# The last directly computed projection of an encoder layer becomes two seven-product units, and the attention steps beside it are packed closer

## The chip, the cores and the metric

The kernel runs on one core of a Trainium2 chip. The metric is the device time of one execution in microseconds. Before the change it is 2159.87 us, the median of 3 runs (2159.56 to 2159.9).

The engines carry these names in the profile: PE (TensorE, matrix products; PEld its weight loads), DVE (VectorE), ACT (ScalarE), POOL (GpSimd, which here mostly issues DMAs) and SP (SyncE, which only issues DMAs).

## The reference

One layer of an encoder, 512 tokens, width 2048, all in float32:

```python
h = rmsnorm(x, attn_norm_w)
aq, ak, av, gq, gk, gv, gr, glr = split(h @ w_in)        # widths 1024 x3, 512, 512, 1024, 1024, 32
attn = mixture_of_dilations(aq, ak, av, rel_table)       # 16 heads x 64: softmax over a banded set of keys + bias
o = gla_forward(gq, gk, gv, glr) + gla_backward(...)     # 4 "linear" heads, dk=128, dv=256, chunked scan with gates
gla_out = rmsnorm_per_head(o) * gla_norm_w * silu(gr)
x = x + concat(attn, gla_out) @ w_out
h = rmsnorm(x, ffn_norm_w)
x = x + (silu(h @ w_gate) * (h @ w_up)) @ w_down         # hidden width 5632
return rmsnorm(x, final_norm_w)
```

The part that matters here is the projection `h @ w_in`, and in it the columns of `gq` and `gk`, 512 each: the queries and keys of the four linear heads.

## The kernel before, in words

**Products.** Every float32 product is made of three products of rounded parts: each operand is split into a high part `hi` (a rounded copy, by ACT) and a low part `lo` (the rest, by DVE), and `hi*hi + hi*lo + lo*hi` is summed in PSUM. The kernel has two ways to compute a projection.

- A *direct job* (`job`, `run_job`) makes 512 output columns for 512 tokens. It goes over the 16 slices of the inner dimension; for each it loads a weight slice (`Stream.load`, on SP), splits it (`Stream.split` on ACT, `Stream.rests` on DVE), and for each of four PSUM banks issues three matmuls of 128x512. That is 16 x 4 x 3 = 192 matmuls a job. Between the banks it advances *side work* by steps: `rate` steps for one slice, taken from a queue of generators (`run_side`). One `yield` in such a generator ends one step.
- A *seven-product unit* (`Feed`, `Front`) makes 256 output columns for 512 tokens by a scheme of Strassen's kind: seven products of block sums in place of eight. A unit has four pieces, a piece has 14 products, and each of these is one matmul of 128x512 (L1562) and one of 128x256 (L1548). The sums of weight blocks (`Blocks.sums`) and the parts (`Blocks.split`) cost DVE and ACT time ahead of it; afterwards `evac7` puts the seven results together with ACT copies, DVE additions and four accumulating DMAs from GpSimd.

**Order of the program around the change.** First two direct jobs make the values `av` (to 104 us). Then `Front.run` computes 14 units: four of `gr`, one each of the first 256 columns of `gq` and `gk`, and eight of `aq` and `ak` (104 to 378 us). Then come three direct jobs: one of kind "A" for the other 256 columns of `gq` and of `gk` (lines L337 to L339), and two of kind "B" for `gv` (L346 to L348). Beside these three jobs, as side work at `RATES[0]` = 3.1 steps a slice, the gates' low-rank projection and then the whole of `attention` are done. After them come the direct jobs of `w_out` at 4.0 steps a slice (603 to 831 us), beside which `gla` computes the linear heads; then the feed-forward layer in seven-product units (`Feed`, to 1695 us) and in `Down`.

**The attention generator.** It has 64 *units of attention* `u` (16 heads, 4 blocks of 128 queries), and 71 iterations of two steps each, since the stages of a unit are spread over iterations like a pipeline. For unit `u`: in iteration `u`, first step, PE makes the scores (`att_scores`, L630 and L631); in the second step DVE adds the bias and finds the extreme (`att_max`, L640). In iteration `u+1`, first step, ACT takes the exponential (`att_exp`, L648). In iteration `u+2`, second step, DVE takes the reciprocal of the sum (L651) and, for even `u`, scales the tile by it (L653). In `u+3`, first step, ACT scales the tile for odd `u` (L657); second step: PE transposes it (L662). In `u+4`, ACT rounds the transposed tile (`att_round`, L670) in the first step, DVE takes the rest (`att_rest`, L676) in the second. Then come the product with the values (L686, L687), `att_lift` (ACT, L696) and `att_mix` (DVE, L705). Every engine works through its own queue in the order in which the instructions were written. Four of the eight PSUM banks belong to the direct job; the attention units share the other four, so the scores of a unit need a bank that DVE has emptied.

**Queries and keys.** `aq` and `ak` lie in DRAM (`qkd`). For each pair of heads `read_qk` (L569) issues eight DMAs from the GpSimd queue, all at once in the iteration with `u % 8 == 1`; `load_qk` then makes their parts on ACT (L592) and DVE (L588), four times each for eight units of attention.

**Linear heads.** `evac_gqk` (L854 to L859) scales the results of the job of kind "A" and stores them in `gqd`; the first 256 columns come from the units through `gfd`. `load_gla` reads them back from GpSimd's queue.

## Time and profile before

| what | value |
|---|---|
| median of 3 runs | 2159.87 us |
| profiled execution | 2159.02 us, of which the span of instructions is 2157.2 us |
| granted PE clock in that execution | 0.999 |
| PE busy | 2145.5 us, 99% of the span |
| DVE, ACT, POOL busy | 1843.6, 1234.4 and 364.0 us |

PE's busy time counts a matmul until its modelled end, and matmuls overlap, so their own rate is read from the distance between the starts of neighbours. DVE and ACT instructions that follow one another overlap a little too: the sum of the durations of a group of them is some per cent more than the busy time of the engine. A time of idleness that is put down to a releaser ("<-PE ps L631") says whose end came last before the waiting instruction started.

### The profile page before, as it was taken

What the parts mean: (1) busy time and instruction counts of PE and PEld (TensorE: products, weight loads), DVE (VectorE), ACT (ScalarE), POOL (GpSimd) and SP (SyncE); (2) the same over time, 40 slices, a digit from 0 to 9 for tenths busy, and PEclk for the clock granted to TensorE, in tenths of its full rate; (3) what the DMA queues carried; (4) which work ended last, traced back from release to release, by engine and by line L of the source; (5) the groups of instructions that cost most, each with busy time, mean ns of one, the idle gap of its engine ahead of it and who ended that gap; (6) DMA issues with size and microseconds to landing.
All of it is one profiled execution on the core that took longest, in us unless ns stands there. A gap on an engine that the chain in (4) does not pass through costs nothing.

```text
span 2157.2 us, 35082 instructions
## 1 busy us (share of the span) xinstructions
PE 2145.5 (99%) x12714; PEld 1896.6 (88%) x12714; DVE 1843.6 (85%) x3187; ACT 1234.4 (57%) x2250; POOL 364.0 (17%) x501
## 2 busy tenths in 40 slices
PE   9999999999999999999999999999999999999998
PEld 7888888888888889888888888888888899999987
DVE  6699999688878788899999998999989888888885
ACT  8455555578876456455555555555555655555562
POOL 0011222211121110022112211221122220021300
PEclk9999999999999999999999999999999999999999
DMA  6367778846575863567677667776677885576982
GB/s 203 136 181 182 179 179 192 245 143 190 174 220 172 279 243 103 149 181 182 181 179 196 173 183 182 178 194 174 180 188 181 260 212 178 179 183 156 282 309 78
DMA packets 266203, 407.55 MB, mean 189 GB/s; under 512 B 19309, under 2 KB 163613, under 8 KB 266030
## 3 DMA queue, kind: packets, MB, share of 16 engines
q1 hardware_dynamic: 206238, 274.59, 39.8%
q0 software_dynamic: 59472, 130.19, 27.1%
q8 instruction: 100, 1.64, 0.3%
q14 instruction: 73, 0.60, 0.1%
q10 hardware_dynamic: 320, 0.53, 0.1%
HBM read 287.47 MB, written 66.39 MB: 164 GB/s over the span
## 4 chain that ended last, share of the span: by engine, by line
PE 56%; DMA 1%; issue 1%; DVE 1%; POOL 0%; ACT 0%; DVEq 0%; ACTq 0%; POOLq 0%
PE ps L1562 25%; PE ps L1548 12%; PE ps L1926 5%; PE ps L1927 5%; PE ps L1925 5%; PE ps L346 1%; PE ps L348 1%; PE ps L347 1%; PE ps L2122 1%; PE ps L2121 1%; PE ps L2120 1%; DMA gd<-b 1%; DMA b<-a 0%; POOL xd L1806 0%; DVE b L1471 0%
## 5 line engine op out<-in xcount | busy, mean ns | idle before, releaser
L1466 ACT CAST b<-b 128x1024 fp32r<-128x1024 f32 (+1 forms) x585 | 533.8, 944 | 386.4 <-DVE b L1471 193.1
L1471 DVE TENSOR_TENSOR b<-b,b 128x1024 fp32r<-128x1024 f32 (+1 forms) x585 | 614.0, 1084 | 34.4 <-ACT b L1466 22.9
L1562 PE MATMUL ps<-b,b 128*128 128x512 f32 x1708 | 500.7, 393 | 0.4 <-ACT b L1466 0.2
L1562 PE MATMUL ps<-a,b 128*128 128x512 f32 x1428 | 418.7, 393 | 0.3 <-DVE b L1582 0.2
L1562 PEld LDWEIGHTS ps<-b,b 128*128 128x128 f32 x1708 | 289.4, 188 | 32.6 <-ACT b L1466 0.6
L1548 PEld LDWEIGHTS ps<-b,b 128*128 128x128 f32 x1708 | 280.6, 190 | 40.8
L1548 PE MATMUL ps<-b,b 128*128 128x256 f32 x1708 | 307.4, 280 | 0.0
L1548 PEld LDWEIGHTS ps<-a,b 128*128 128x128 f32 x1428 | 236.9, 189 | 38.0 <-DVE b L1471 0.5
L1562 PEld LDWEIGHTS ps<-a,b 128*128 128x128 f32 x1428 | 238.5, 188 | 24.1 <-issue 0.6
L1548 PE MATMUL ps<-a,b 128*128 128x256 f32 x1428 | 256.6, 280 | 0.1
L1453 DVE TENSOR_TENSOR b<-b 128x512 f32<-128x512 f32 x268 | 183.6, 685 | 19.0 <-PE ps L1927 7.3
L1926 PE MATMUL ps<-b,b 128*128 128x256 f32 x624 | 176.6, 283 | 0.0
L1927 PE MATMUL ps<-b,b 128*128 128x256 f32 x624 | 176.6, 283 | 0.0
L1925 PE MATMUL ps<-b,b 128*128 128x256 f32 x624 | 176.6, 283 | 0.0
L346 PE MATMUL ps<-b,b 128*128 128x512 f32 x332 | 133.8, 403 | 0.1
L348 PE MATMUL ps<-b,b 128*128 128x512 f32 x332 | 129.8, 391 | 0.1
L347 PE MATMUL ps<-b,b 128*128 128x512 f32 x332 | 129.5, 390 | 0.0
L1454 DVE TENSOR_TENSOR b<-b,b 128x256 f32<-128x256 f32 x268 | 114.0, 425 | 9.3
L1455 DVE TENSOR_TENSOR b<-b,b 128x256 f32<-128x256 f32 x268 | 114.0, 425 | 9.2
L1927 PEld LDWEIGHTS ps<-b,b 128*128 128x128 f32 x624 | 119.8, 192 | 0.0
L1925 PEld LDWEIGHTS ps<-b,b 128*128 128x128 f32 x624 | 119.8, 192 | 0.0
L1926 PEld LDWEIGHTS ps<-b,b 128*128 128x128 f32 x624 | 119.8, 192 | 0.0
(308 smaller groups left out, 4039.8 us busy)
## 6 DMA issues: line engine op xcount, KB each, us to landing
b<-in_w_gate_dram SPq DMA_DIRECT2D x109, 512.0 KB, 3.7
b<-in_w_up_dram SPq DMA_DIRECT2D x88, 512.0 KB, 3.8
b<-in_w_down_dram SPq DMA_DIRECT2D x88, 512.0 KB, 5.4
b<-in_w_in_dram SPq DMA_DIRECT2D x86, 512.0 KB, 3.8
b<-a POOLq DMA_DIRECT2D x168, 256.0 KB, 4.5
b<-in_w_out_dram SPq DMA_DIRECT2D x32, 512.0 KB, 6.3
gd<-b POOLq DMA_DIRECT2D x22, 512.0 KB, 4.0
b<-gd SPq DMA_DIRECT2D x22, 512.0 KB, 8.3
```

What stands on the lines that cost most here:

```text
L346: mm(o, xh.t[:, c], wh.t[:, w], start=first and not on, stop=False, skip_group_check=on)
L347: mm(o, xh.t[:, c], wl.t[:, w], start=False, stop=False, skip_group_check=on)
L348: mm(o, xl.t[:, c], wh.t[:, w], start=False, stop=last, skip_group_check=on)
L1453: dve.tensor_tensor(s_[:, :, 0:2], r[:, :, 1:3], r[:, :, 0:1].to_broadcast(shape), op=OP.add)
L1454: dve.tensor_tensor(s_[:, :, 2], s_[:, :, 0], r[:, :, 2], op=OP.add)
L1466: act.copy(o, src)
L1471: dve.tensor_tensor(o, src, h, op=OP.subtract)
L1548: mm(o, wl, xh, start=False, stop=end, skip_group_check=True)
L1562: mm(o.rearrange("p (s t) -> p s t", s=2), wh, x_, start=first and p == 0, stop=False, skip_group_check=True)
L1925: mm(o, xh[:, t], wh, start=first and h == 0, stop=False, skip_group_check=True)
L1926: mm(o, xh[:, t], wl, start=False, stop=False, skip_group_check=True)
L1927: mm(o, xl[:, t], wh, start=False, stop=last, skip_group_check=True)
```

## The change

- **Projection.** The direct job of kind "A" and `evac_gqk` are gone. `Front` has two more units, the second 256 columns of `gq` and of `gk`, as its units 6 and 7; `aq` and `ak` follow. So there are 16 units and then two direct jobs (`gv`). `gfd` has four parts, and `load_gla` reads all heads from it.
- **Rate.** `RATES[0]`, the steps of side work for one slice in the jobs of `gv`, is 4.4 in place of 3.1. The generators `low_rank` and `attention`, and `load_qk(0)`, `load_v(0)` and the late store of the last unit, hang on the first job of `gv`.
- **Scaling.** `att_norm` is called for unit `u-1` at the end of the second step of iteration `u` (before: for `u-2`, at the head of the second step), and `att_scale` for `u-2` (before `u-3`). Who multiplies the tile by the reciprocal: ACT for `u % 4 == 2`, and for odd `u` below 8; GpSimd for the other odd units, 28 in number; DVE for `u % 4 == 0`. Before, DVE had the 32 even ones and ACT the 32 odd ones.
- **Transfers.** `read_qk` is a generator that issues one DMA and yields; `attention` calls it twice an iteration, from `u % 8 == 0` on, so that the eight DMAs of a pair lie in four iterations. `scan_operands` (two memsets and four DMAs on GpSimd) is paced in the same way and starts at `u == 43` in place of 47.

```diff
                         for r in (slice(0, 64), slice(64, 128)):
                             pool.dma_start(out=qkr[pr][i][n].f[r], in_=src)
+                            yield
...
         def att_norm(u):
             dve.reciprocal(ar[u % 4], asum[u % 4])
-            if u % 2 == 0:
-                dve.tensor_scalar(AT[u].t, AT[u].t, ar[u % 4], None, op0=OP.mult)
+            if not by_act(u):
+                e = pool if u % 2 else dve
+                e.tensor_scalar(AT[u].t, AT[u].t, ar[u % 4], None, op0=OP.mult)
+
+        def by_act(u):
+            return u % 4 == 2 or u % 2 and u < 8
 
         def att_scale(u):
-            if u % 2:
+            if by_act(u):
                 act.activation(AT[u].t, AT[u].t, AF.Copy, scale=ar[u % 4])
...
-                    if u % 8 == 1:
-                        read_qk(h // 2 + 1)
+                    if u % 8 == 0:
+                        for _ in reads:
+                            pass
+                        reads = read_qk(h // 2 + 1)
+                    next(reads, None)
...
                 run(att_scores, u)
-                run(att_scale, u - 3)
+                run(att_scale, u - 2)
                 run(att_round, u - 4)
                 run(att_exp, u - 1)
...
                 yield
-                run(att_norm, u - 2)
+                next(reads, None)
                 run(att_transpose, u - 3)
...
                     run(att_mix, (u - 7) // 2, UNITS // 2)
+                run(att_norm, u - 1)
...
-        RATES = (3.1, 4.0)
+        RATES = (4.4, 4.0)
         APART = 12
-        seg = [(w_in, C_GQ + 256), (w_in, C_GK + 256)]
-        job("A", [piece512(seg, None, k) for k in range(0, KT, 2)], list(range(KT)), acts_h,
-            evac_gqk, rate=RATES[0], start=gstart, before=before_first, limit=3)
         for pr in range(2):
             j = job("B", [piece512(w_in, C_GV + pr * 512, k) for k in range(0, KT, 2)], list(range(KT)), acts_h,
-                    evac_gv(pr), rate=RATES[0],
-                    before=(lambda i: load_gates() if i == 12 else None) if pr else None)
+                    evac_gv(pr), rate=RATES[0], start=None if pr else gstart, limit=3,
+                    before=(lambda i: load_gates() if i == 12 else None) if pr else before_first)
...
                 self.units = [(w_in, C_GR + g * 256) for g in range(4)] + [(w_in, C_GQ), (w_in, C_GK)] + \
+                    [(w_in, C_GQ + 256), (w_in, C_GK + 256)] + \
                     [(w_in, c + g * 256) for g in range(4) for c in (C_AQ, C_AK)]
...
-                    if u == 4:
+                    if u in (4, 6):
                         dve.scalar_tensor_tensor(c_.t, c_.t, P ** -0.5, r, op0=OP.mult, op1=OP.mult)
                     else:
                         dve.tensor_tensor(c_.t, c_.t, r, op=OP.mult)
-                    pool.dma_start(out=grd[u] if u < 4 else gfd[u - 4] if u < 6 else qkd[u - 6], in_=c)
+                    pool.dma_start(out=grd[u] if u < 4 else gfd[u - 4] if u < 8 else qkd[u - 8], in_=c)
```

In the tables of instruction order below, a row gives the line, the operation, what it writes and reads (`a` and `b` are SBUF tiles of 512 and 1024 columns, `ps` PSUM banks, `small` the per-row numbers) and its size. After the change L641 is `att_max`, L652 and L655 are `att_norm`, L681 is `att_rest`, L710 is `att_mix`.

In DVE's queue, two units of attention in the middle of that stage, before:

```order
L651 RECIPROCAL small<-small 128x1
L653 TENSOR_SCALAR a_252_4969<-a_252_4969,small 128x512
L676 TENSOR_TENSOR b_496_5023<-ps_198_5004,b_495_5022 128x4x128
L640 ISA a_263_5052,small<-ps_199_5018,b_488_4864 128x512
L640 ISA small 128x1
L651 RECIPROCAL small<-small 128x1
L676 TENSOR_TENSOR b_496_5023<-ps_200_5037,b_495_5022 128x4x128
L640 ISA a_265_5077,small<-ps_202_5060,b_488_4864 128x512
L640 ISA small 128x1
L705 TENSOR_TENSOR a_251_4932<-ps_201_5042,a_264_5065 64x2x128
```

The same place in DVE's queue after the change:

```order
L681 TENSOR_TENSOR b_541_5230<-ps_205_5237,b_540_5229 128x4x128
L641 ISA a_250_5274,small<-ps_207_5260,b_536_5147 128x512
L641 ISA small 128x1
L710 TENSOR_TENSOR a_243_5211<-ps_206_5242,a_249_5265 64x2x128
L652 RECIPROCAL small<-small 128x1
L655 TENSOR_SCALAR a_248_5252<-a_248_5252,small 128x512
L218 TENSOR_TENSOR a_241_5198<-b_526_4910,a_240_5197 128x512
L681 TENSOR_TENSOR b_544_5293<-ps_208_5268,b_543_5292 128x4x128
L641 ISA a_253_5315,small<-ps_209_5289,b_536_5147 128x512
L641 ISA small 128x1
```

The rest and the maximum now stand ahead of the reciprocal, and of two scalings by DVE in four units one is left.

In GpSimd's queue, the stores of the direct job's results and the reads of a pair of heads, before:

```order
L859 DMA gqd<-a_219_4669 128x512
L569 DMA a_222_4685<-qkd 64x512 x2
L569 DMA a_223_4686<-qkd 64x512 x2
L569 DMA a_224_4687<-qkd 64x512 x2
L569 DMA a_225_4688<-qkd 64x512 x2
```

After the change, in GpSimd's queue where its first scaling stands (that of unit 9):

```order
L569 DMA a_186_4679<-qkd 64x512 x2
L569 DMA a_187_4680<-qkd 64x512 x2
L569 DMA a_188_4681<-qkd 64x512 x2
L655 ISA
L655 TENSOR_SCALAR a_192_4737<-a_192_4737,small 128x512
L569 DMA a_189_4682<-qkd 64x512 x2
L655 TENSOR_SCALAR a_197_4802<-a_197_4802,small 128x512
L655 TENSOR_SCALAR a_206_4869<-a_206_4869,small 128x512
L569 DMA a_215_4946<-qkd 64x512 x2
L655 TENSOR_SCALAR a_213_4936<-a_213_4936,small 128x512
```

Scalings now stand between the DMA issues, and ahead of the first of them there is one instruction without operands (the row `L655 ISA`), by which GpSimd loads the code that the scaling needs. It stands there once in the program.

33 lines of the change are left out of this document (13 added, 20 removed).

## The prediction

> **What bounds the kernel now.** I read the page's busy times first, then the table by stretches, since the change touches two stages only.
>
> ```profile
> PE 2145.5 (99%) x12714; PEld 1896.6 (88%) x12714; DVE 1843.6 (85%) x3187; ACT 1234.4 (57%) x2250; POOL 364.0 (17%) x501
> ...
> 104.00:377.00 273.00, 272.73 (x1564) 239.14 (x1563) 251.28 (x399) 143.94 (x236) 57.65 (x74) 1.00 0.74 183
> 399.00:596.00 197.00, 196.84 (x1095) 167.39 (x1094) 166.68 (x395) 155.00 (x330) 35.08 (x67) 1.00 0.57 172
> 596.00:831.00 235.00, 234.15 (x1142) 196.61 (x1141) 184.00 (x392) 139.20 (x308) 39.77 (x69) 1.00 0.68 221
> ```
>
> The columns are the stretch, its length, and the busy times of PE, PEld, DVE, ACT and POOL; then clock, DMA share, GB/s. The three stretches are the front units, the attention beside direct jobs, and the linear heads beside `w_out`. PE is without a pause in all of them, at full clock. So a matmul saved is time saved, as long as the others keep up: DVE is at 92% in the front (251.28 of 273), at 85% in the attention (166.68 of 197), ACT there at 79%.
>
> How fast matmuls follow each other stands in the timeline, which gives starts. Two matmuls of the direct job that goes away with one between them, two of a later direct job with twenty between them, and the first matmuls of the first and of the last front unit:
>
> ```profile
> 380.00 0.39 PE L337 MATMUL ps<-b,b 128*128 128x512 f32 x1
> ...
> 380.46 0.39 PE L339 MATMUL ps<-b,b 128*128 128x512 f32 x1
> ...
> 610.65 0.40 PE L346 MATMUL ps<-b,a 128*128 128x512 f32 x1
> ...
> 615.42 0.39 PE L346 MATMUL ps<-b,a 128*128 128x512 f32 x1
> ...
> 104.24 0.62 PE L1562 MATMUL ps<-b,b 128*128 128x512 f32 x2
> ...
> 358.45 0.63 PE L1562 MATMUL ps<-b,b 128*128 128x512 f32 x2
> ```
>
> A direct matmul takes 0.23 us from start to start ((380.46 - 380.00) / 2); over 21 of them it is (615.42 - 610.65) / 21 = 0.227, which I use, since the longer row rounds less. A front unit takes (358.45 - 104.24) / 13 = 19.55 us.
>
> **Term 1: PE.** Away go 192 direct matmuls: 192 x 0.227 = 43.6 us. New are two units: 2 x 19.55 = 39.1 us. Everything else on PE (scores, transposes, values, low-rank) keeps its count. Sum: -4.5 us. Its bounds are narrow: with 0.23 a matmul it is -5.1, and the pauses of a unit are already in 19.55.
>
> **Term 2: the front with 16 units.** DVE and ACT get two more units' sums, parts and `evac7`; they are the same per unit as now, at 92% of DVE, where PE is busy 272.73 of 273 us. Cost 0: covered by PE's own 39.1 us.
>
> **Term 3: the attention in less time.** This decides. The 64 units start here:
>
> ```profile
> L630 PE MATMUL ps<-a,a x64: 389/393/467, 399.0 to 595.3; 128*128 128x512 f32 x64
> ```
>
> That is 196.3 / 63 = 3.12 us a unit. By the instruction order 492 direct matmuls lie between the first and the last score now, 351 with the change (4.4 steps a slice, not 3.1). So PE needs 141 x 0.227 = 32.0 us less: 164.3 us, 2.61 us a unit. The work of the others beside it, in the rows of that stretch:
>
> ```profile
> L640 DVE CUSTOM_DVE_ANT_0 a<-ps,b 128x512 f32<-128x512 f32 x64 | 43.9, 686 | 18.2 <-PE ps L631 18.1
> L676 DVE TENSOR_TENSOR b<-ps,b 128x512 fp32r<-128x512 f32 x60 | 41.0, 684 | 7.8 <-ACT b L670 7.2
> L588 DVE SCALAR_TENSOR_TENSOR a<-a,a 64x512 fp32r<-64x512 f32 (+1 forms) x28 | 19.2, 686 | 0.7 <-ACT a L592 0.4
> L218 DVE TENSOR_TENSOR a<-b,a 128x512 fp32r<-128x512 f32 x25 | 17.1, 683 | 0.1
> L653 DVE TENSOR_SCALAR a<-a,small 128x512 f32<-128x512 f32 x31 | 15.1, 487 | 1.1
> L218 DVE TENSOR_TENSOR b<-b,b 128x512 fp32r<-128x512 f32 x18 | 12.2, 686 | 0.2
> L651 DVE RECIPROCAL small<-small 128x1 f32<-128x1 f32 x62 | 9.7, 157 | 0.3
> L880 DVE TENSOR_SCALAR b<-ps,small 128x512 f32<-128x512 f32 x2 | 1.5, 750 | 2.6 <-PE ps L348 2.6
> L854 DVE SCALAR_TENSOR_TENSOR a<-ps,a 128x512 f32<-128x512 f32 x2 | 1.3, 682 | 0.0
> ...
> L670 ACT CAST b<-ps 128x512 fp32r<-128x512 f32 x60 | 35.1, 586 | 32.4 <-PE ps L662 31.8
> L657 ACT ACTIVATE a<-a,small 128x512 f32<-128x512 f32 x31 | 22.3, 719 | 3.9 <-DVE small L651 3.8
> L237 ACT CAST a<-b 128x512 fp32r<-128x512 f32 x24 | 14.7, 611 | 0.1
> L882 ACT ACTIVATE b<-ps,small 128x512 f32<-128x512 f32 x2 | 1.3, 689 | 0.0
> ...
> L569 POOL DMA_DIRECT2D a<-qkd x52 | 27.9, 545 | 60.6 <-DVE a L705 44.6 <-ACT a L592 3.9 <-DMA b<-a 2.4
> ```
>
> DVE loses 15 scalings (31 to 16, 0.487 each: 7.3 us), 11 weight parts (43 to 32, 0.684: 7.5) and the four operations of `evac_gqk` (L854, L857, 0.682: 2.7), and gets two more of `evac_gv` (0.750: 1.5): 166.7 - 16.0 = 150.7 us of 164.3, 92%. ACT loses 11 scalings (31 to 20, 0.719: 7.9) and 9 copies of weights (0.611: 5.5) and gets two of `evac_gv` (0.689: 1.4): 155.0 - 12.0 = 143.0, 87%. So both fit, with 13.6 us to spare on DVE, the same share at which PE does not wait in the front. The largest idle times of both are waits for PE (L640 for the scores, L670 for the transposes): they follow PE. The rest and the maximum, which empty the banks that the next scores need, now stand ahead of the reciprocal and the scaling in DVE's queue, 0.157 + 0.487 us sooner. I take 0.0 for this term, as in the front; its upper end is in the rivals.
>
> **Term 4: GpSimd.** Its 28 scalings have no row. The nearest that writes such a tile is a memset:
>
> ```profile
> L1032 POOL MEMSET a<- x8: 526/552/1597, 635.3 to 712.1; 128x512 f32 x8
> ```
>
> So 0.55 to 1.60 us each; I take 1.0, since a scaling also reads. GpSimd's queue then holds 35.1 - 2.2 (`gqd`) + 28 x 1.0 = 61 us in 164: not full. Behind a scaling wait the DMA issues of `read_qk`, paced at 2 in 2.6 us (2 x 0.545); their data are wanted iterations later. Ahead of it stand at most two of them. The reciprocal comes at the end of iteration u+1 and the transposes in the middle of u+3: 1.5 x 2.61 = 3.9 us, less 1.1 for two issues leaves 2.8, more than 1.60. PE does not wait: 0. ACT's scalings have a step more than they need: 0.
>
> The Trainium skill has a price here (GPSIMD Engine Reference, section 3.1): it gives 769 ns for a tight loop over 512 elements, which lies inside my two ends. No run so far shows it.
>
> **Term 5: the shift behind it.** Attention now ends 24 direct matmuls later relative to the jobs of `w_out` (by the order the last transpose of the linear heads stands at matmul 435 of 480, before at 411), 5.4 us less of 15.7 us of reserve. What it holds up, the last head's parts, is wanted at matmul 456 (21 x 0.227 = 4.8 us later). 0. `scan_operands` comes four units sooner, its DMAs a step apart: 0.
>
> **Sum.** -4.5 + 0 + 0 + 0 + 0 on the profiled execution: 2159.02 - 4.5 = 2154.5. The median is 0.85 above that execution, so 2155.4.
>
> **Rivals.**
>
> *GpSimd holds up DVE (slower).* Nothing in this trace shows GpSimd reading SBUF beside DVE. If each scaling kept DVE waiting for its whole length, DVE would lose 28 x 0.55 to 28 x 1.60 = 15 to 45 us, with 13.6 to spare: PE then waits 1.8 to 31 us. It decides from 13.6 / 28 = 0.49 us a scaling. At 1.0 us it gives 2155.4 + 28 - 13.6 = 2169.8. Against it: only part of DVE's work could be hit. The operations with two SBUF inputs are L588 and L218, 48.5 of 166.7 us, 29%; then the loss is 4 to 13 us and fits into the reserve.
>
> The Trainium skill has this as a rule (SBUF — State Buffer, on the port pair that VectorE and GpSimd share): the pair is an exclusive lock, held for a whole instruction, against VectorE operations with two SBUF inputs when GpSimd reads SBUF, and against its 2-port modes. By that rule the smaller loss above holds, and the time would stay 2155.4.
>
> *DVE and ACT hand over too slowly (no change).* Where ACT scales (u % 4 == 2), it now waits for the reciprocal just made, then scales (0.719) and rounds (0.586) before DVE can take the rest (0.684), the maximum (0.686) and the next reciprocal (0.157): 2.83 us round against 2.61 a unit. If the other three units don't win it back, 16 x 0.22 = 3.5 us; in the first eight units, six by ACT, four more rounds, 0.9. The gain would be gone: 2159.8. Against it: DVE now waits for the rounding only 7.2 us over 60 rests (row L676), 0.12 each.
>
> *The first scaling comes late (no change).* Ahead of it GpSimd loads code. By the order it gets there after six DMA issues that wait for the scores of unit 7, 3.3 us behind them; PE wants unit 9 at 5.5 x 2.61 = 14.4 us behind them. A load of up to 10 us is free, each microsecond above costs one, once. The trace has no such load; I keep 0 to 5 us: 2155.4 to 2160.4.
>
> The Trainium skill (GPSIMD Engine Reference, section 2.1) gives about 6 us for the first call of freshly loaded code; by that it would be hidden.
>
> *More is won.* Pauses of the attention (0.16 us by the row above) and of the linear heads (0.85) go, and matmuls count 0.23: 2155.4 - 1.0 - 0.6 = 2153.8.
>
> **How the numbers follow.** A difference of 0.2% (4.3 us) is about what a measurement of this kernel tells from none, so my forecast lies at its edge.
>
> - PE stays the bound: 0.50, of which 0.40 faster by over 0.2% and 0.10 within.
> - Hand-overs: 0.20, 0.17 within, 0.03 slower.
> - GpSimd holds up DVE: 0.20, 0.17 slower, 0.03 within.
> - Late first scaling: 0.06, 0.04 within, 0.02 slower.
> - More is won: 0.04, faster.
>
> Together 0.44 faster, 0.34 within, 0.22 slower. The range is 2153.8 to 2167.0: below lies 0.02, above the dearer half of the GpSimd rival, some 0.12.
>
> **What would show it.** Term 1: 19.5 us from unit to unit in the front, now 16, and the first scores some 35 us later (39.1, less the 18 direct matmuls, 4.1 us, that stand ahead of them no more). Term 3: 2.6 us between scores, PE busy over 99% of that stretch; wrong, if waits of PE for L681 or L641 appear and scores stand 2.8 us or more apart. Term 4: the duration of L655 on POOL, no wait of PE for it; wrong, if PE's transposes wait for POOL. The GpSimd rival: L218 and L589 longer, or DVE pauses in front of them. Late code: a single gap of PE at unit 9.

## The result, and the profile after

The changed kernel takes 2167.36 us, the median of 6 runs (2165.22 to 2167.8). The kernel before took 2159.72 us beside it, the median of its 6 runs. The ratio is 1.0034 with a 95% interval of 1.0021 to 1.0047, so the change is slower by 0.34%. The forecast was 2155.4 us; the result lies 12 us above it and just above the range.

The profiled execution of the changed kernel took 2165.22 us, 10.7 more than the 2154.5 that the sum gave for it. First the busy times of the page:

```profile
PE 2146.3 (99%) x12746; PEld 1894.2 (88%) x12746; DVE 1860.3 (86%) x3209; ACT 1238.5 (57%) x2256; POOL 422.9 (20%) x535
```

They hardly differ from before. The table by stretches does; its columns are those of the table by stretches in the prediction, and the stretches are the front with 16 units, the attention, and the linear heads beside `w_out`:

```profile
104.60:417.00 312.40, 312.10 (x1791) 273.80 (x1790) 288.12 (x458) 164.96 (x271) 65.62 (x84) 1.00 0.74 183
434.00:610.00 176.00, 169.94 (x957) 140.31 (x956) 152.29 (x368) 143.37 (x312) 88.68 (x99) 1.00 0.60 183
610.00:845.00 235.00, 234.44 (x1169) 197.50 (x1168) 187.01 (x402) 139.08 (x313) 43.75 (x73) 1.00 0.68 219
```

PE is without a pause in the first and the third stretch and idle for 6 of 176 us in the second. The timeline gives the first matmuls of the first and the last front unit:

```profile
104.55 0.62 PE L1559 MATMUL ps<-b,b 128*128 128x512 f32 x2
...
397.76 0.63 PE L1559 MATMUL ps<-b,b 128*128 128x512 f32 x2
```

That is (397.76 - 104.55) / 15 = 19.55 us a unit, to the hundredth what term 1 took. The instructions of the line that makes the scores, and what its matmuls and weight loads together waited for (us, times):

```profile
L631 PE MATMUL ps<-a,a x64: 387/395/506, 434.8 to 609.4; 128*128 128x512 f32 x64
...
  DVE b L681: 14.2, 25
```

The scores spread over 174.6 us in place of 164.3, that is 2.77 us a unit and not 2.61. These 10.3 us are all but 0.4 of what is missing. Of them PE shows 6.1 us as idle in the stretch. The rest fits what each pause hides. Of the 25 waits above 9 are those of matmuls, shown below, and 16 those of weight loads; in PE's timeline 16 scores start late. A matmul is drawn 0.39 us long although the next can start after 0.23, so the first 0.16 us of a pause is not seen as idle. Behind a pause the second matmul of the scores starts 0.34 us after the first and not 0.23 (606.08 and 606.42 us). 16 x (0.16 + 0.11) makes 4.3 us, an estimate from these rows.

Who holds PE up stands in PE's waits between 420 and 620 us (total, times, longest):

```profile
PE ps L631 <- DVE b L681: 4.1, 9, 0.8
PE ps L631 <- DVE b L880: 1.5, 1, 1.5
PE ps L838 <- DVE a L832: 0.4, 1, 0.4
PE ps L667 <- DVE b L880: 0.2, 1, 0.2
```

The kernel before has one wait in the same part of the program:

```profile
PE ps L662 <- DVE b L880: 0.2, 1, 0.2
```

And why DVE's rest (L681) is late stands in the groups of that stretch, by line (L641 maximum, L681 rest, L589 and L218 low parts of queries, keys and weights; on ACT L662 scaling, L675 rounding; on POOL L655 scaling):

```profile
L641 DVE CUSTOM_DVE_ANT_0 a<-ps,b 128x512 f32<-128x512 f32 x63 | 43.0, 683 | 5.2 <-PE ps L632 5.2
L681 DVE TENSOR_TENSOR b<-ps,b 128x512 fp32r<-128x512 f32 x60 | 41.2, 687 | 13.6 <-ACT b L675 13.0
L589 DVE SCALAR_TENSOR_TENSOR a<-a,a 64x512 fp32r<-64x512 f32 (+1 forms) x28 | 21.1, 752 | 2.1 <-ACT a L593 1.6
L675 ACT CAST b<-ps 128x512 fp32r<-128x512 f32 x60 | 34.7, 578 | 3.2 <-PE ps L667 2.9
L662 ACT ACTIVATE a<-a,small 128x512 f32<-128x512 f32 x19 | 13.7, 723 | 19.8 <-DVE small L652 19.7
L655 POOL TENSOR_SCALAR a<-a,small 128x512 f32<-128x512 f32 x27 | 50.6, 1876 | 68.6 <-DVE small L652 55.1 <-PE ps L632 10.2 <-PE ps L692 3.0
```

Before, ACT's rounding waited 31.8 us for PE: it followed PE. Now it waits 2.9 us for PE, and the scaling ahead of it in ACT's queue waits 19.7 us for the reciprocal. DVE's rest waits 13.0 us for the rounding, nearly twice the 7.2 of before, though DVE has less work. DVE's wait for the scores has shrunk from 18.1 to 5.2 us: DVE no longer follows PE, PE follows DVE. One such place, from the timeline of all engines:

```profile
485.98 0.60 PE L667 MATMUL ps<-idn,a 128*128 128x128 f32 x4
...
486.69 0.17 DVE L652 RECIPROCAL small<-small 128x1 f32<-128x1 f32 x1
...
486.95 0.72 ACT L662 ACTIVATE a<-a,small 128x512 f32<-128x512 f32 x1 [1.87 <-DVE small L652]
...
487.58 0.57 ACT L675 CAST b<-ps 128x512 fp32r<-128x512 f32 x1
...
488.18 0.69 DVE L681 TENSOR_TENSOR b<-ps,b 128x512 fp32r<-128x512 f32 x1 [1.32 <-ACT b L675]
...
488.79 0.68 DVE L641 CUSTOM_DVE_ANT_0 a<-ps,b 128x512 f32<-128x512 f32 x1
...
489.39 0.16 DVE L652 RECIPROCAL small<-small 128x1 f32<-128x1 f32 x1
```

The reciprocal is the last thing that DVE does in its step. ACT stands idle for 1.87 us until it comes, then scales, and only then rounds a tile whose transposes (L667) had ended at 486.58 us, 1.0 us before the rounding starts. DVE, its own step ended, waits 1.32 us for that rounding. The rest and the maximum, which empty the banks for the next scores, are late by as much.

GpSimd is not in this chain. Its scalings take 1.88 us each, and no wait of PE names them.

### The profile page after: what moved, and what is told of

Same layout as the page of the kernel before. It is cut to its first block, busy times and chain, and to the rows that moved or that the text cites. A ratio compares the mean times of both kernels' runs of the same rounds, so it can differ in the third digit from the quotient of the medians.

```text
span 2163.5 us, 35263 instructions
## 1 busy us (share of the span) xinstructions
PE 2146.3 (99%) x12746; PEld 1894.2 (88%) x12746; DVE 1860.3 (86%) x3209; ACT 1238.5 (57%) x2256; POOL 422.9 (20%) x535
## 4 chain that ended last, share of the span: by engine, by line
PE 91%; DVE 4%; ACT 2%; DMA 2%; issue 1%; POOL 0%; DVEq 0%; ACTq 0%; POOLq 0%
PE ps L1559 34%; PE ps L1545 17%; PE ps L346 5%; PE ps L348 5%; PE ps L347 5%; PE ps L1925 5%; PE ps L1926 5%; PE ps L1924 5%; DMA b<-a 1%; PE ps L667 1%; PE ps L2121 1%; PE ps L2120 1%; PE ps L2119 1%; PE ps L1569 1%; PE ps L1568 1%
## 5 line engine op out<-in xcount | busy, mean ns | idle before, releaser
L1463 ACT CAST b<-b 128x1024 fp32r<-128x1024 f32 (+1 forms) x601 | 548.9, 944 | 402.3 <-DVE b L1468 213.3
L1468 DVE TENSOR_TENSOR b<-b,b 128x1024 fp32r<-128x1024 f32 (+1 forms) x601 | 630.8, 1085 | 31.8 <-ACT b L1463 20.5
L1559 PE MATMUL ps<-b,b 128*128 128x512 f32 x1760 | 517.3, 393 | 0.4 <-ACT b L1463 0.2
L1559 PE MATMUL ps<-a,b 128*128 128x512 f32 x1488 | 436.5, 394 | 0.3 <-ACT b L1463 0.3
L1559 PEld LDWEIGHTS ps<-b,b 128*128 128x128 f32 x1760 | 298.2, 189 | 33.1 <-ACT b L1463 0.7
L1545 PEld LDWEIGHTS ps<-b,b 128*128 128x128 f32 x1760 | 289.9, 190 | 42.3
L1545 PE MATMUL ps<-b,b 128*128 128x256 f32 x1760 | 318.1, 280 | 0.0
L1545 PEld LDWEIGHTS ps<-a,b 128*128 128x128 f32 x1488 | 246.6, 189 | 39.1 <-DVE b L1468 0.5
L1559 PEld LDWEIGHTS ps<-a,b 128*128 128x128 f32 x1488 | 249.0, 189 | 25.4 <-ACT b L1463 0.5
L1545 PE MATMUL ps<-a,b 128*128 128x256 f32 x1488 | 267.6, 281 | 0.0
L1925 PE MATMUL ps<-b,b 128*128 128x256 f32 x624 | 176.7, 283 | 0.0
L1926 PE MATMUL ps<-b,b 128*128 128x256 f32 x624 | 176.7, 283 | 0.0
L1924 PE MATMUL ps<-b,b 128*128 128x256 f32 x624 | 176.7, 283 | 0.0
L346 PE MATMUL ps<-b,b 128*128 128x512 f32 x352 | 142.5, 405 | 0.0
L348 PE MATMUL ps<-b,b 128*128 128x512 f32 x352 | 137.8, 392 | 0.0
L347 PE MATMUL ps<-b,b 128*128 128x512 f32 x352 | 137.6, 391 | 0.0
L1604 POOL DMA_DIRECT2D b<-a x58 | 50.2, 866 | 412.5 <-ACT b L1463 238.2
L1452 DVE TENSOR_TENSOR b<-b,b 128x256 f32<-128x256 f32 x276 | 117.4, 426 | 9.5
L1451 DVE TENSOR_TENSOR b<-b,b 128x256 f32<-128x256 f32 x276 | 117.4, 425 | 9.6
L1924 PEld LDWEIGHTS ps<-b,b 128*128 128x128 f32 x624 | 119.8, 192 | 0.0
L1925 PEld LDWEIGHTS ps<-b,b 128*128 128x128 f32 x624 | 119.8, 192 | 0.0
```

Of the source, the lines that this page charges most:

```text
L346: mm(o, xh.t[:, c], wh.t[:, w], start=first and not on, stop=False, skip_group_check=on)
L347: mm(o, xh.t[:, c], wl.t[:, w], start=False, stop=False, skip_group_check=on)
L348: mm(o, xl.t[:, c], wh.t[:, w], start=False, stop=last, skip_group_check=on)
L1451: dve.tensor_tensor(s_[:, :, 2], s_[:, :, 0], r[:, :, 2], op=OP.add)
L1463: act.copy(o, src)
L1468: dve.tensor_tensor(o, src, h, op=OP.subtract)
```

## The experiments

The theory that the trace suggests is **A**: the place of ACT's scaling. Written ahead of the rounding and for a unit whose reciprocal has only just been made, it holds up the rounding, and that the rest, the maximum and PE. The rivals are **B**, that GpSimd's scalings hold up DVE, and **C**, that DVE and ACT simply have too much work at 2.61 us a unit. All medians below are of 5 to 11 runs, the ratios stand against 27 to 33 runs of the kernel before on the same chip. The experiments ran on four chips, so where two sections are compared, the ratios are the safer measure.

### ACT's scaling an iteration later, or behind the rounding

```diff
-                run(att_scale, u - 2)
+                run(att_scale, u - 3)
                 run(att_round, u - 4)
                 run(att_exp, u - 1)
```

> The changed kernel with one edit: ACT's scaling is called for u-3, an iteration later, as it was before the change; who scales, the rate and everything else stay as changed. Theory A (hand-over: ACT's scaling stands ahead of its rounding and waits for the reciprocal that DVE made last of all): the idle time of the rests (L681) for the rounding falls from 13.6 us to about 7, PE's waits for L681 (9 of them, 4.1 us) go, the scores come 2.61 to 2.67 us apart, and the time falls by 4 to 10 us, to 2156 to 2163 us. Theory B (GpSimd's 28 scalings hold up DVE) and theory C (the work of DVE and ACT is simply too dense at 2.61 us a unit): nothing is taken from either, so the scores stay 2.75 us or more apart and the time within 2 us of the changed kernel's.

```diff
-                run(att_scale, u - 2)
                 run(att_round, u - 4)
                 run(att_exp, u - 1)
+                run(att_scale, u - 2)
```

> The changed kernel with one edit: ACT's scaling keeps its unit (u-2) but is written behind ACT's rounding and exponential of the step, not ahead of them. Theory A: what counts is what stands behind the waiting scaling, so this does as much as putting it an iteration later: idle time of the rests about 7 us, time 2156 to 2163 us. If it is the age of the reciprocal alone that counts and not the place in the queue, ACT would still wait for it, but nobody behind it: the same. Theories B and C: 2 us at most from the changed kernel.

The first gives 2160.52 us (ratio 1.0005, 0.9996 to 1.0013), the second 2160.86 (1.0003, 0.9994 to 1.0012). Both win 6.5 to 7 us on the change as it was. The scores of the second, and its groups in the same stretch:

```profile
L631 PE MATMUL ps<-a,a x64: 389/397/501, 436.4 to 604.7; 128*128 128x512 f32 x64
...
L681 DVE TENSOR_TENSOR b<-ps,b 128x512 fp32r<-128x512 f32 x62 | 42.5, 686 | 4.7 <-ACT b L675 3.7
...
L675 ACT CAST b<-ps 128x512 fp32r<-128x512 f32 x62 | 36.0, 581 | 11.2 <-PE ps L667 10.9
L662 ACT ACTIVATE a<-a,small 128x512 f32<-128x512 f32 x20 | 14.2, 710 | 0.0
```

ACT's scaling no longer waits for the reciprocal (19.7 us in the change), the rest's wait for the rounding falls from 13.0 to 3.7 us, and the scores take 168.3 us in place of 174.6. The second edit leaves unit, engine and amount of work as they are and moves the scaling by two places in one queue. So A is shown, at some 6.5 us of the 12 that are missing; by B and C the two edits could have won 2 us at most.

### The old scaling at the new pace

The units, the rate of 4.4 and the paced transfers stay; the scaling is that of the kernel before, without GpSimd:

```diff
-                e = pool if u % 2 else dve
-                e.tensor_scalar(AT[u].t, AT[u].t, ar[u % 4], None, op0=OP.mult)
+                dve.tensor_scalar(AT[u].t, AT[u].t, ar[u % 4], None, op0=OP.mult)
...
-            return u % 4 == 2 or u % 2 and u < 8
+            return u % 2
...
-                run(att_scale, u - 2)
+                run(att_scale, u - 3)
...
                 next(reads, None)
+                run(att_norm, u - 2)
...
-                run(att_norm, u - 1)
```

> The changed kernel's units, rate of 4.4 steps and paced transfers, but the scaling as before the change: the reciprocal for u-2 at the head of the second step, DVE scales the even units, ACT the odd ones at u-3, GpSimd none. This takes away both the hand-over of theory A and all of GpSimd's work, and gives DVE 16 and ACT 12 scalings more (7.8 and 8.6 us of some 176). Theory A: 2156 to 2162 us, better or as good as with ACT's scaling later. Theory B: the same gain. Theory C (too dense): DVE at 150.7 + 7.8 of 164.3 us and ACT at 143.0 + 8.6 are now at 96 and 92%, so it is no faster than the changed kernel, 2165 us or more.

It gives 2163.24 us (1.0017, 1.0008 to 1.0026): better than the change by 4 us, worse than the first two by 2.5. So the shared scaling of the change is worth something at this pace, once its place in ACT's queue is right. A's numbers (2156 to 2162) and C's (2165 or more) both miss; the value lies between. So something besides A has a part, and the new pace costs 3.6 us even with the old scaling; that this is density is not shown here.

### GpSimd's share given to DVE

```diff
-                e = pool if u % 2 else dve
-                e.tensor_scalar(AT[u].t, AT[u].t, ar[u % 4], None, op0=OP.mult)
+                dve.tensor_scalar(AT[u].t, AT[u].t, ar[u % 4], None, op0=OP.mult)
```

> The changed kernel with one edit: the 28 scalings of GpSimd go to VectorE, and all else stays. Theory B: whatever GpSimd's scalings cost DVE (L589 was 752 ns in place of 686, some single ones 1.1 us) goes, but DVE gets 28 x 0.49 = 13.7 us of own work; B at its full size (28 x 1.85 us) would make it 2 us faster or more. Theory A and C: DVE is busier by 13.7 us of 176, the hand-over to ACT stays, so it is slower, by 2 to 10 us: 2169 to 2177 us.

2171.96 us (1.0057, 1.0044 to 1.0069), slower than the change by 4.6 us. B would have made it faster. The scores of this kernel, and the stretch of the attention in it:

```profile
L631 PE MATMUL ps<-a,a x64: 387/397/505, 434.9 to 615.6; 128*128 128x512 f32 x64
```

```profile
434.00:610.00 176.00, 167.42 (x932) 136.12 (x931) 156.20 (x381) 139.46 (x301) 37.60 (x70) 1.00 0.61 178
```

The scores spread over 180.7 us, 6.1 more than in the change, while 28 x 0.49 = 13.7 us were put on DVE: at this pace nearly half of what is put on DVE reaches PE.

### The parts at the old pace

GpSimd's 28 scalings and the paced transfers alone, in the kernel before (its direct job, its 3.1 steps, its places):

```diff
-            if u % 2 == 0:
-                dve.tensor_scalar(AT[u].t, AT[u].t, ar[u % 4], None, op0=OP.mult)
+            if not by_act(u):
+                e = pool if u % 2 else dve
+                e.tensor_scalar(AT[u].t, AT[u].t, ar[u % 4], None, op0=OP.mult)
+
+        def by_act(u):
+            return u % 2 and u < 8
```

> The kernel before, with its direct job of kind A, its 3.1 steps a slice and its places for the scaling, but GpSimd scales the odd units from 8 on (28 of ACT's 32) and the transfers are one a step as in the change. This shows GpSimd's scalings alone, at 3.12 us a unit. Theory B (they hold up DVE): in the worst case DVE loses 28 x 1.85 = 52 us of the 29 that it has to spare beside the attention, and the time rises by 5 us or more. Theory A and C: GpSimd is off the path and ACT is relieved, so the time stays within 2 us of the kernel before, and the scores 3.12 us apart.

The whole new scaling and the transfers, but still the direct job and 3.1 steps:

```diff
+            return u % 4 == 2 or u % 2 and u < 8
...
-                run(att_scale, u - 3)
+                run(att_scale, u - 2)
...
-                run(att_norm, u - 2)
...
+                run(att_norm, u - 1)
```

> The kernel before with only the second half of the change: the scaling shared by the three engines a step sooner and the transfers one a step, but still the direct job of kind A and 3.1 steps a slice. Theory A says that the hand-over makes a round of 2.83 us or somewhat more in the steps with u % 4 == 2, against 3.12 us a unit here, so it costs little: within 2 us of the kernel before, with idle time of the rests for the rounding of 13 us or more all the same. If the new scaling costs by itself, whatever the pace, the time rises by 5 us or more.

The first gives 2159.72 us (1.0004, 0.9995 to 1.0013), the second 2159.16 (1.0000, 0.9992 to 1.0009): no difference in either. The groups of the second beside the attention show why that is no acquittal:

```profile
L641 DVE CUSTOM_DVE_ANT_0 a<-ps,b 128x512 f32<-128x512 f32 x64 | 43.7, 683 | 11.6 <-PE ps L632 11.3
L681 DVE TENSOR_TENSOR b<-ps,b 128x512 fp32r<-128x512 f32 x60 | 41.4, 690 | 19.3 <-ACT b L675 18.5
...
L662 ACT ACTIVATE a<-a,small 128x512 f32<-128x512 f32 x19 | 13.8, 724 | 23.7 <-DVE small L652 23.7
```

The bad hand-over is there in full. The rest waits 18.5 us for the rounding, more than in the change, and the scores still come 3.11 us apart (398.5 to 594.6 us), and nothing is lost: at that pace DVE has room (it is busy 162.98 of 197 us). The 6.5 us of A need both halves of the change; the new pace alone, with the old scaling, cost 3.6 us in the section before.

### A slower pace

After A, the version with the scaling behind the rounding still needs 168.3 us for the scores where PE's work makes 164.3. Is that density? Two variants of that version spread the attention over more direct matmuls:

```diff
-        RATES = (4.4, 4.0)
+        RATES = (4.2, 4.2)
```

> ACT's scaling behind the rounding as in the experiment that wrote it so (2160.86 us; there the scores came 168.3 / 63 = 2.67 us apart where 164.3 / 63 = 2.61 were due), and the rates 4.2 and 4.2 in place of 4.4 and 4.0. By the order of instructions 366 direct matmuls in place of 351 then lie between the first and the last score, so PE has 3.4 us more work there and the sum of PE's work is the same. Theory C' (what is left is density: with DVE at 91% each delay of DVE or ACT reaches PE): half or more of the 4 us left goes, 2157 to 2159 us. If what is left has another cause, a fixed cost of each unit or of the jobs' ends: 2160 to 2162 us.

```diff
-        RATES = (4.4, 4.0)
+        RATES = (4.0, 4.4)
```

> As the experiment with the rates 4.2 and 4.2, but 4.0 and 4.4: 381 direct matmuls between the first and the last score, 2.72 us a unit by PE's work (171.1 us). The last transpose of the linear heads stands at matmul 432 of 480 (435 with 4.4 and 4.0), so these keep their reserve by their place, though their steps are denser by a tenth. Theory C': nearly all of the 4 us goes and the forecast's 2155 to 2157 us are reached. If the linear heads can't take 4.4 steps a slice, their stage is longer by what the attention wins: 2159 to 2162 us.

Both miss: 2164.76 us (1.0024, 1.0013 to 1.0034) and 2163.01 (1.0016, 1.0007 to 1.0025). PE's waits from the attention to the end of the linear heads, of the one with 4.0 and 4.4:

```profile
PE ps L1037 <- DVE a L1043: 2.0, 1, 2.0
PE ps L667 <- ACT b L882: 1.1, 1, 1.1
PE ps L1037 <- DVE a L1002: 0.9, 1, 0.9
PE ps L346 <- DVE b L1324: 0.8, 1, 0.8
```

With 4.0 and 4.4 no wait of PE for L681 is left, and the scores take 173.2 us where 171.1 are due: the attention is nearly clean. But the linear heads (L1037) and the jobs of `w_out` beside them (L346, for L1324) now run at 4.4 steps and wait 3.7 us. With 4.2 and 4.2 there are still 3.4 us of waits for L681, and the scores take 173.9 us where 167.7 are due; why this rate is worse than 4.4 is not shown. A rate shifts what falls beside what, and so it is no clean test of density.

### Taking work off DVE

A cleaner test: in the version with the scaling behind the rounding, DVE's 16 scalings are left out (their tiles stay unscaled), or given to GpSimd.

```diff
-            if not by_act(u):
+            if not by_act(u) and u % 4:
                 e = pool if u % 2 else dve
```

> The kernel with ACT's scaling behind the rounding (2160.86 us), and DVE's 16 scalings (u % 4 == 0) are left out: those tiles of the attention stay unscaled. All else is there. DVE has 16 x 0.49 = 7.8 us less to do in the 168.3 us between the first and the last score, 86% in place of 91. Theory C' (what is left of the loss is DVE's density): the waits of PE for L681 that are left in 575 to 605 us go, the attention takes 165 to 166.5 us, and the time is 2157 to 2159 us. If what is left comes from something else (ACT in the first eight units, the jobs' ends), 2160 us or more.

```diff
-                e = pool if u % 2 else dve
+                e = pool if u >= 8 else dve
```

> The same kernel, complete, but GpSimd takes DVE's scalings from unit 8 on too: 42 scalings of 1.85 us in place of 28, 78 us, beside some 35 us of DMA issues in 168 us. Theory C': as when they are left out, 2157 to 2159 us, if GpSimd keeps pace (three units running are its own: 3 x 1.85 + 6 x 0.545 = 8.8 us of 3 x 2.61 = 7.8 us, so it falls behind by 1 us of the 2.8 that it has and catches up at the unit that ACT scales). Theory B: 14 more scalings that hold up DVE's two-input operations, so no gain or a loss, 2161 us or more, and waits of PE's transposes for POOL.

2159.11 us without them (0.9998, 0.9989 to 1.0007), 2159.92 with GpSimd doing them (1.0000, 0.9991 to 1.0009). I compare three stretches of the attention, from 10, 25 and 140 us after the first score, 15, 115 and 32 us long. The version with the scaling behind the rounding, all with PE's busy time first:

```profile
446.00:461.00 15.00, 14.01 (x77) 11.04 (x76) 12.42 (x29) 12.89 (x28) 3.65 (x7) 1.00 0.79 227
461.00:576.00 115.00, 114.83 (x674) 98.30 (x673) 104.55 (x254) 97.71 (x215) 67.54 (x72) 1.00 0.60 177
576.00:608.00 32.00, 31.04 (x175) 25.25 (x174) 30.72 (x72) 27.87 (x61) 12.34 (x9) 1.00 0.57 206
```

And that with 42 scalings on GpSimd:

```profile
444.00:459.00 15.00, 15.00 (x91) 12.94 (x90) 14.25 (x36) 14.02 (x31) 4.49 (x7) 1.00 0.74 211
459.00:574.00 115.00, 114.75 (x670) 98.32 (x669) 99.66 (x242) 97.26 (x215) 83.75 (x85) 1.00 0.59 178
574.00:606.00 32.00, 31.82 (x183) 26.23 (x182) 29.99 (x69) 27.80 (x60) 19.33 (x13) 1.00 0.59 195
```

In the last stretch DVE is at 96% in the first of them (30.72 of 32), and PE is idle for 0.96 us; with the scalings given to GpSimd it is 0.18 us, left out 0.20. In the middle there is next to nothing to win. Other profiles agree: 0.97 and 1.01 us in two more of this version's variants in which DVE has these scalings, 0.18 and 0.19 in three in which GpSimd has them. So DVE's density costs about a microsecond, at the end of the attention, by the profiles. The medians can't show it: the ratios 1.0003, 0.9998 and 1.0000 lie within each other's intervals, and neither median reached the 2157 to 2159 us of theory C'. The profiled execution with 42 scalings on GpSimd needs 165.4 us for the scores and took 2155.70 us, the forecast's time. But that is the lowest of its 11 times, and the median is 4.2 us higher.

### The first stretch

The first stretch loses 0 to 3 us, differently from profile to profile. The idea was that ACT has six of the first eight scalings. In the version with the scaling behind the rounding:

```diff
-                e = pool if u % 2 else dve
+                e = pool if u % 2 and u >= 8 else dve
...
-            return u % 4 == 2 or u % 2 and u < 8
+            return u % 4 == 2
```

> The same kernel, but DVE and not ACT scales the odd units below 8: ACT has 4 x 0.72 us less in the first eight units, where DVE stands idle (8.8 of 12 us busy between 442 and 454 us). Theory: the three waits of PE at 448.9, 451.6 and 457.7 us (0.54, 0.50 and 0.42 us) come from ACT, which has six of the first eight scalings; then they go, and the time is 1 to 1.5 us lower, 2159 to 2160 us. If they come from the start of the attention itself, nothing changes.

With that alone it is 2159.49 us (1.0004, 0.9996 to 1.0013), together with the 42 on GpSimd 2158.99 (1.0000, 0.9991 to 1.0008):

> GpSimd has the scalings with u % 4 == 0 from 8 on and DVE the odd ones below 8, ACT only those with u % 4 == 2, written behind its rounding. If both causes hold, both gains add: 2155.5 to 2158 us, the forecast of the change, and faster than the kernel before by 0.1% or more. If GpSimd with 42 scalings is too slow, 2161 us or more.

In the first of these the first stretch is no better (1.76 us idle, 0.99 without the edit), so ACT's scalings are not its cause, and that the median lies in the range expected, 2159 to 2160 us, is luck. The second misses its 2155.5 to 2158. What goes with it is another row. ACT makes the high parts of the next pair's queries and keys (L593), read back from DRAM, and this is where it stood, from the timelines of the version with the scaling behind the rounding and of the one with the scaling an iteration later:

```profile
447.17 0.63 ACT L593 ACTIVATE a<-a 128x512 fp32r<-128x512 f32 x1 [1.93 <-DMA a<-qkd]
```

```profile
449.13 0.63 ACT L593 ACTIVATE a<-a 128x512 fp32r<-128x512 f32 x1 [3.65 <-DMA a<-qkd]
449.66 0.71 ACT L662 ACTIVATE a<-a,small 128x512 f32<-128x512 f32 x1
```

ACT waits for the transfer, with scaling and rounding behind it. In the second of these profiles more is lost than the pause: PE is idle for 2.59 us behind this wait, and then its matmuls from 451.71 to 453.85 us start 0.43 us apart in place of 0.23, at a granted clock of 0.89 in that first stretch. All other profiles have 1.00 there, that with the old scaling too, where PE is idle for 3.08 us.

In ten of the fifteen profiles with 16 front units ACT waits there 0.67 to 3.66 us for the second pair of heads, and PE is idle for 0.52 to 3.08 us of the first stretch; in the five others it waits 0 to 0.52 us, and PE is idle for at most 0.09. Before the change ACT waits for no transfer beside the attention. There GpSimd issues the reads of the second pair from 3.2 us ahead of the first score to 4.9 us behind it, and ACT comes to them 9.8 us behind it. In the changed kernel they are issued one a step, behind the store of the last front unit, 2.4 to 7.3 us after the first score, and ACT comes to them 9 us after it. So in four kernels the second pair's parts are made from `u == 5` on, two an iteration:

```diff
-                    if u % 8 == 4 and h // 2 + 1 < NH // 2:
+                    if u == 5:
+                        urgent.append(load_qk(1))
+                    if u > 8 and u % 8 == 4 and h // 2 + 1 < NH // 2:
                         urgent.append(slow(load_qk(h // 2 + 1)))
```

With 42 scalings on GpSimd:

> The version with 42 scalings on GpSimd (2159.92 us, its profiled execution 2155.7), and the parts of the second pair of heads (L593 and L589) are made from u = 5 on, two an iteration, not from u = 4 on, one an iteration; the other pairs as they were. Theory: in many executions ACT waits there for the read from DRAM, and the rounding behind it makes PE wait 2 to 3 us; then this gives 2156 to 2158 us with a spread of 3 us between executions in place of 6, and no wait of L593 after 440 us. If the spread comes from elsewhere (the pauses of the front units), the median stays at 2159 to 2160 us.

In the change as it was made:

> The change as it was made with this one edit: the parts of the second pair of heads from u = 5 on, two an iteration. Theory: of the 12 us between the forecast and the result some 2 are of this kind (the pauses of 0.2 to 0.6 us at 448 to 459 us), so 2164.5 to 2166 us; the waits for L681 later in the attention stay, about 7 us. If the first eight units are slow for the reason of the others (ACT's scaling ahead of the rounding), no gain: 2167 us.

With the scaling behind the rounding:

> ACT's scaling behind the rounding (2160.86 us) with the parts of the second pair from u = 5 on. Theory: 1.5 to 2 us less, 2158.5 to 2159.5 us, the attention 166.5 to 167 us long; what is then left is DVE's density at 575 to 605 us. Otherwise 2160 to 2161 us.

With 42 on GpSimd and the first odd units on DVE:

> As the first, but the odd units below 8 are scaled by DVE and not by ACT, which has the parts of the second pair closer together now. Theory: at least as good as the first, 2156 to 2158 us, and faster than the kernel before by 0.05 to 0.15%. If the parts, closer together, hold up the rounding of u = 5 to 7 themselves, both stay at 2159 us or more.

| kernel | without | with parts from `u == 5` | ratio to before, without | ratio to before, with |
|---|---|---|---|---|
| 42 on GpSimd | 2159.92 | 2158.62 | 1.0000 | 1.0000 (0.9991 to 1.0008) |
| the change | 2167.36 | 2166.11 | 1.0034 | 1.0034 (1.0022 to 1.0047) |
| scaling behind the rounding | 2160.86 | 2159.68 | 1.0003 | 1.0003 (0.9994 to 1.0012) |
| 42 on GpSimd, DVE the first odd ones | 2158.99 | 2158.87 | 1.0000 | 0.9999 (0.9990 to 1.0008) |

All four medians are lower, by 0.1 to 1.3 us, and all four lie 0.1 to 0.9 us above the ranges expected. But against the kernel before on the same chip the ratios differ by 0.0001 at most, so no gain is shown. In three of them the wait is not gone (0.5 to 1.3 us); where it is gone, in the version with the scaling behind the rounding, the first stretch is clean (15.00 of 15 us busy). In the change as it was made that stretch is no better (2.12 us idle, before 1.72): there the hand-over of theory A remains. The spread with 42 on GpSimd fell from 6.2 to 4.5 us (2156.54 to 2160.99) and not to the 3 expected. So the late transfer is a wait that goes with the loss of the first stretch in the profiles; its price in the medians is not shown, and it is not the whole reason why they lie above the best profiles.

**What stays open.** Of the 12 us the place of ACT's scaling is 6.5. About 1 is DVE's density at the end and about 1 the first stretch, both by the profile with the scaling behind the rounding alone; the remaining 3 or so are not placed. The best complete versions take 2158.62 and 2158.87 us, not to be told from the kernel before; a version faster than that was not found. The profiled execution of the second (2156.47 us) has 166.0 us of scores, 1.7 more than due, and a wait of 0.4 us at the low-rank part. The 2.4 us between that execution and its median I could not place. The front units differ from profile to profile (311.6 to 315.3 us from the first to the last matmul of 16 units, over 15 kernels, where PE waits up to 1.1 us at a time for DVE's `evac7`), which may be part of it. That applies to 14 units too (272.7 to 275.2 us in three profiles), so it takes nothing from the difference.

## Why the prediction was wrong

**Term 1, PE's 4.5 us: right.** 19.55 us a unit in the front, now 16 of them; the first scores came 35.8 us later, as said (some 35).

**Term 2, the front: right.** PE is busy 312.10 of 312.40 us.

**Term 5, the shift behind it: right.** PE is busy 234.44 of 235 us beside the linear heads. The profile with 42 scalings on GpSimd, the lowest of that version's executions, comes near the sum without term 3: with scores 1.1 us over due it took 2155.70 us, where the sum gave 2154.5.

**Term 3, the attention in less time, taken as 0.0: this step failed.** It measured 10.3 us in the profiled execution. The loads that it added up came out right: 150.7 us were foretold for DVE and 143.0 for ACT, over 164.3 us, and the stretch of 176 us shows 152.29 and 143.37. What was wrong is the conclusion from them. That the largest idle times of both are waits for PE, so that "they follow PE", was true of the kernel before, and the change ended it by where it put an instruction. Moving the reciprocal behind the maximum made the banks free sooner, as said, but it also put ACT's scaling ahead of a rounding that was ready.

**The rival "hand over too slowly" named the place, the order and the round; its price was too small.** It gave 2159.8 us with a chance of 0.20. The round is about as computed: in the rows at 486 us it takes 489.39 - 486.69 = 2.70 us from reciprocal to reciprocal. But I set it against the mean of 2.61 us a unit, 0.22 us each. The pace is not even. Starts of four scores in a row, from PE's timeline of the version with the scaling behind the rounding:

```profile
486.94 0.40 PE L631 MATMUL ps<-a,a 128*128 128x512 f32 x1
...
489.48 0.40 PE L631 MATMUL ps<-a,a 128*128 128x512 f32 x1
...
491.76 0.40 PE L631 MATMUL ps<-a,a 128*128 128x512 f32 x1
...
495.00 0.39 PE L631 MATMUL ps<-a,a 128*128 128x512 f32 x1
```

They are 2.54, 2.28 and 3.24 us apart, since the products with the values come in every second iteration only, and the direct matmuls do not fall evenly between the steps. A round of 2.7 us that meets 2.28 can cost more than the mean lets one expect. But the short distances alone are not the reason: the kernel before has 13 of 63 under 2.4 us too, and so has the one with the whole new scaling at 3.1 steps, which has the same hand-over and loses nothing; in the version shown it is 30 of 63. How much comes from the mean and how much from the unevenness is not shown. Measured, the place of ACT's scaling costs 6.5 us, where 3.5 + 0.9 stood.

**Two more parts had been put at nothing:** in term 3 the density of DVE, about 1 us at the end by the profiles, and in term 4 the transfers "wanted iterations later". The reads of the second pair now come later and the iterations have become short, so that ACT waits for them in ten profiles, at a price that the medians don't show. The second gv job, which now ends inside the attention, holds up PE's scores by another 1.5 us (the wait for L880); with the scaling behind the rounding it is 0.4.

**Term 4, GpSimd's scalings: right in effect, wrong in size.** A scaling takes 1.56 to 2.45 us, 1.88 in the mean, which is above the upper end of 1.60 that I had taken. PE still does not wait for it, because 2.8 us were free. The Trainium skill's 769 ns (GPSIMD Engine Reference, section 3.1) is half of the shortest one here.

**The rival "GpSimd holds up DVE": its smaller form was right.** DVE's parts beside it (L589) are longer by (752 - 686) x 28 = 1.8 us in all, less than the 4 to 13 us of that form and inside the reserve; as an effect on the time, nothing was measured. Its 48.5 us of operations with two SBUF inputs left out L751 and L808, 6.2 us in the same rows, which changes nothing in this.

**The late first scaling did not happen.** GpSimd was there ahead of it and waited 4.10 us for the reciprocal, so any loading of code lay within that time:

```profile
463.27 1.56 POOL L655 TENSOR_SCALAR a<-a,small 128x512 f32<-128x512 f32 x1 [4.10 <-DVE small L652]
```

In the last version of the table above (42 on GpSimd, DVE the first odd ones, parts from `u == 5`) the first scaling starts 1.2 us after GpSimd's configuring instructions for it (456.7 and 457.9 us). So loading took no longer there than that, and not some 6 us.

**The chances.** That DVE would be at 92%, "the same share at which PE does not wait in the front", was the argument for 0.50 on PE staying the bound. The same share is not the same stage: the attention is a ring over four banks and three engines, in which a delay of one can come back to it. The 0.22 that I gave to slower was too little for a chain that I had found myself and priced at the mean.

## What to carry to other kernels

In a software pipeline, an instruction that waits for a result just made belongs behind everything on its queue that is already ready; the busy shares cannot show this, only the order of the queue beside the step that makes the result. A ring of hand-overs priced against the mean iteration was priced too low here, 4.4 us for 6.5, so give such a price more room and look at the single distances too. When a pipeline is packed closer, look again at each read from DRAM whose lead was counted in iterations. A part of a change that costs nothing at the old pace is not thereby free at the new one.

## What the runs showed of the hardware

GpSimd and DVE slow each other where both read SBUF. In the profile with GpSimd's scalings at the old places, where DVE's rest and maximum (one input from PSUM) run beside them, the groups are:

```profile
L655 POOL TENSOR_SCALAR a<-a,small 128x512 f32<-128x512 f32 x28 | 44.6, 1592 | 106.5 <-DVE small L652 84.9 <-ACT a L649 11.7 <-ACT a L701 9.8
...
L589 DVE SCALAR_TENSOR_TENSOR a<-a,a 64x512 fp32r<-64x512 f32 (+1 forms) x28 | 19.2, 686 | 0.8 <-ACT a L593 0.4
```

With the scalings a step sooner, at the same pace, they fall beside operations of two SBUF inputs and are 1912 and 801 ns. In the changed kernel, one such place in DVE's timeline, and GpSimd's:

```profile
473.01 0.67 DVE L761 TENSOR_TENSOR a<-a,a 128x512 fp32r<-128x512 f32 x1
473.60 0.69 DVE L218 TENSOR_TENSOR a<-b,a 128x512 fp32r<-128x512 f32 x1
474.20 1.10 DVE L589 SCALAR_TENSOR_TENSOR a<-a,a 128x512 fp32r<-128x512 f32 x1
```

```profile
473.26 2.37 POOL L655 TENSOR_SCALAR a<-a,small 128x512 f32<-128x512 f32 x1 [3.74 <-DVE small L652]
```

The first of DVE's operations runs into the start of GpSimd's one, the other two lie inside it. The first two keep their 0.67 to 0.69 us, the third takes 1.10, and GpSimd takes 2.37 in place of 1.56. The Trainium skill (SBUF — State Buffer, section on the two separate sides) has an exclusive lock here, held for a whole instruction by whoever starts first, with the other engine fully blocked. GpSimd's loss fits that: its 0.8 us more are about the time until DVE's second operation ends, 1.03 us after GpSimd's start. DVE's loss does not: a hold to the end of GpSimd's instruction, at 475.63 us, would not let L589 end at 475.30. In the changed kernel's trace six of DVE's operations that lie inside a scaling are lengthened, to between 0.98 and 1.10 us, and each ends 0.33 or 0.34 us ahead of the drawn end of GpSimd's. So one meeting costs DVE some 0.3 to 0.4 us and GpSimd up to 0.9, and DVE is not blocked for the whole length.
